# Four stretches between steps of side tasks changed in a two-layer hybrid decoder step

## The chip, the cores and the metric

The kernel runs on one core of a Trainium2 chip. The metric is device time in microseconds (us) of one execution: the median of three runs for the kernel before.

## What is computed

One inference step of a decoder with two layers, for a prompt of 1024 positions and 8 sample rows, here side by side as T = 1032 columns, with D = 1024 channels in fp32. The core of the reference:

```
def layer(x, c, pos, s_ret, conv_buf, w_ada, b_ada, g_mix, w_in, ...):
    mod = jax.nn.silu(c) @ w_ada + b_ada
    sh1, sc1, gt1, sh2, sc2, gt2 = jnp.split(mod, 6, axis=-1)
    h = modulate(rmsnorm(x, g_mix), sh1, sc1)
    p = h @ w_in                       # q, k, v, g: 4 heads x 128;  u, vv: 4 groups x 128
    ...
    o, s_new = retention(q, k, v, s_ret)       # chunks of 128: S = g*S + k^T v, o = att v + q S
    o_ret = silu(g) * groupnorm(o)
    o_gm, v_rows = chunk_gmlp(gelu(u), gelu(vv), w_s, b_s, gmlp_ln_gain)
    x = x + gt1 * (concat([o_ret, o_gm]) @ w_out)
    h2 = modulate(rmsnorm(x, g_ffn), sh2, sc2)
    a, buf_new = causal_dwconv(h2 @ w_up, conv_buf, conv_w, conv_b)
    f = silu(a[..., :D_FF]) * a[..., D_FF:]    # D_FF = 2048
    x = x + gt2 * (f @ w_down)
```

## The kernel before

**Matmuls.** Channels lie on the partitions. Every large product is made of 128x128 weights against three column chunks of 344. For precision each operand is split into a high and a low part (hi, lo), and a product is three matmuls into the same PSUM bank: L262 hi·hi, L263 hi·lo, L264 lo·hi, here called a triple. There are 3840 triples in the program, and places in it are told below as the number of triples ahead of them. A weight piece comes by DMA as `raw` (two pieces ahead), ACT makes `hi` of it (L212) and DVE `lo` (L221). Three functions run the triples: `unit()` for one output tile of an input or up projection (24 triples: 3 chunks by 8), `joint()` for the first two tiles after a norm (48), and `partial()` for the output and down projections, whose inputs are products of earlier units. ACT's and DVE's evacuations of a unit (L291, L292) and the split of weights (`W.ahead()`) are issued from inside these loops.

**Side tasks.** Everything else is done by generators in a queue (`Side`, shown below): the retention heads (v, k, q, o), the gMLP groups, the FFN's convolution and product, the norms, and ada (the modulation's products, L573 for the DMA and L589 for PE). Each `yield x` ends a step and says how many modelled microseconds later the next is due. `tick(us)` moves the modelled clock on and runs at most two steps that are due, in the queue's order; ada has a lower priority than heads, norms a higher one. `unit()` and `partial()` call it every three triples with KB = 1.31, `joint()` after each triple with KB/3. So the program order on every engine is fixed when the kernel is built, by these numbers; each engine then works through its own queue in that order. Slots in SBUF (23, one size) and PSUM banks (8) are taken from rotating pools, in program order too.

**The tasks that the change touches.**
- `norm()` (L441 to 468): a norm's side of a joint. `add_squares()` adds up squares on DVE (L377), `inv_rms()` multiplies them by a matrix of ones (L395), then the inverse root goes over DRAM and comes back as R, by which DVE multiplies (L317, L292). The stretch at L444 stands between L377 and L395, for the norms that have a `wait` (the second and the third chunk of a joint).
- `Head.task_k()` (L715 to 756): k is rotated, transposed on PE and copied to `kt` on ACT (L729); after the stretch at L732 PE multiplies kt by vt (L742). The q and o tasks of the head follow: `qm` (L767), the products L772, L782, then o and the mixing of heads (L814, L817, L830, L849).
- `Ffn.evac_b().rest()` (L931 to 940): the second half of an FFN step. After L932 come the three taps of the convolution (L911, L915), after L934 the product with the first half's SiLU (L935, on DVE; L925 is the SiLU), `ahi` (L937, ACT), and 2.5 later `alo` (L939, DVE). ahi and alo are the inputs of the down projection's `partial()`.

Of the kernel before, what the change touches and what calls it, by code (L numbers as in the profile page):

```python
# [90 lines left out]
def tile_hybrid_decoder_step(  # L91
# [321 lines left out]
    def to_dram(w):  # L413
        rd = dp.tile([4, QW], F32, tag="rd", name=f"rd{count[0]}")
        nc.gpsimd.dma_start(out=rd, in_=w[0:128:32])
        return rd

    def from_dram(o, rd):

        nc.sync.dma_start(out=o, in_=rd.rearrange("j n -> (j n)")[0:o.shape[1]].partition_broadcast(128))  # L420
# [17 lines left out]
    def norm(c, hold, R, A, B, gate=None, dma=True, wait=0):  # L438

        n = CW if c < 2 else CW - NB  # L440
        if wait:  # L441
            yield wait
        rows = add_squares(c, hold, gate)
        yield 5 if wait else 4  # L444
        w = inv_rms(rows)
        yield 4
        if dma:
            rd = to_dram(w)
        if c == 2 or not dma:
            r = spread(w, (3,) if dma else range(4))  # L450
        yield 1
        o = R[:, c * CW:c * CW + n]
        if dma:
            from_dram(o, rd)
        else:
            nc.scalar.activation(out=o, in_=r[:, 0:n], func=ACTF.Copy)
        if c == 2:
            q = small([128, KT, NB], "gs")
            ss = slice(SEQ, T)
            rb = r[:, CW - NB:CW].unsqueeze(1).to_broadcast([128, KT, NB])  # L460
            nc.vector.tensor_tensor(out=q, in0=XS, in1=rb, op=ALU.mult)
            nc.vector.tensor_tensor(out=q, in0=q, in1=A[:, :, 1:9], op=ALU.mult)
            nc.vector.tensor_tensor(out=q, in0=q, in1=B[:, :, 1:9], op=ALU.add)
            nc.scalar.activation(out=Hh[:, :, ss], in_=q, func=ACTF.Copy)
            nc.vector.tensor_tensor(out=Hl[:, :, ss], in0=q, in1=Hhf[:, :, ss], op=ALU.subtract)
# [193 lines left out]
    class Head:  # L659
# [61 lines left out]
        def task_k(self, sw):  # L721
            h = self.h
            yield 3
            self.rope(self.k, sw)
            kt = slot("kt")
            yield 5

            def ev(hf, ps):
                nc.scalar.activation(  # L729
                    out=kt[:, hf * 512:(hf + 1) * 512], in_=ps, func=ACTF.Identity, scale=dec[:, h:h + 1])  # L730
            halves(self.k, ev)
            yield 4  # L732
            vb = self.vb[:, 0:1024]
            vb8 = vb.rearrange("p (b e) -> p b e", b=8)
            nc.gpsimd.tensor_tensor(
                out=vb8, in0=vb8, in1=self.k[:, SEQ:T].unsqueeze(2).to_broadcast([128, 8, 128]), op=ALU.mult)
            self.S = slot("S")
            S = self.S[:, 0:1024].rearrange("p (c e) -> p c e", c=8)
            pss = [sps(), sps()]
            for q in range(8):  # L740
                t = slice(q * 128, (q + 1) * 128)
                nc.tensor.matmul(  # L742
                    pss[q // 4][:, q % 4 * 128:(q % 4 + 1) * 128], kt[:, t], self.vt[:, t], start=True, stop=True)
            for hf, ps in enumerate(pss):
                for q in range(4):
                    c = hf * 4 + q
                    kv = ps[:, q * 128:(q + 1) * 128]
                    if c == 0:
                        nc.vector.tensor_copy(S[:, 0], kv)
                    else:  # L750
                        nc.vector.scalar_tensor_tensor(
                            out=S[:, c], in0=S[:, c - 1], scalar=GAMMA[h] ** 128, in1=kv, op0=ALU.mult, op1=ALU.add)
            yield 3.5
            nc.gpsimd.dma_start(out=rp_o[self.l, h], in_=S[:, 7])
            s0 = self.S0[:, 0:1024]
            nc.vector.scalar_tensor_tensor(out=s0, in0=s0, scalar=GAMMA[h], in1=vb, op0=ALU.mult, op1=ALU.add)
            yield 2
            nc.gpsimd.dma_start(
                out=rs_o[self.l, h], in_=self.S0[:, 0:1024].rearrange("p (b e) -> p b e", b=8))
# [126 lines left out]
    class Ffn:  # L886
# [41 lines left out]
        def evac_b(self, ps, p):  # L928
            ac = self.conv(ps, 16 + p)

            def rest():  # L931
                yield 5  # L932
                c1, c2 = self.c1, (yield from self.taps(ac, 16 + p))
                yield 4  # L934
                nc.vector.tensor_tensor(out=c2[:, 0:T], in0=c2[:, 0:T], in1=c1[:, 0:T], op=ALU.mult)  # L935
                hi, lo = slot("ahi", F32R), slot("alo", F32R)
                nc.scalar.activation(out=hi[:, 0:T], in_=c2[:, 0:T], func=ACTF.Copy)  # L937
                yield 2.5
                nc.vector.tensor_tensor(  # L939
                    out=lo[:, 0:T], in0=c2[:, 0:T], in1=hi.bitcast(F32)[:, 0:T], op=ALU.subtract)  # L940
                self.f[p] = (hi, lo)
            self.tasks[p] = side.add(rest(), after=[self.first])
# [315 lines left out]
```

## Time and profile before

| | us |
|---|---|
| median of 3 runs | 2059.28 (2058.11 to 2060.38) |
| the profiled execution | 2058.09 |
| its span | 2056.4 |
| PE busy | 2021.2 (98%) |
| DVE busy | 1230.2 (60%) |
| ACT busy | 669.4 (33%) |

The program is bound by PE, which works through its matmuls back to back. A part of the profile lists the times in which PE stood idle by the operation that it waited for; a timeline shows the instructions of an engine with their start and length, and in square brackets how long the engine was idle ahead of one and what ended it. Matmul ends are modelled: each is drawn 0.32 long though one starts every 0.16, so distances are best read from start to start.

### The profile page before, as it was taken

To read this page: it belongs to the slowest core of one execution; us is meant where nothing else is said; L and a number is where in the kernel's file an instruction comes from. 1 tells how busy PE (TensorE), PEld (TensorE's weight loads), DVE (VectorE), ACT (ScalarE), POOL (GpSimd) and SP (SyncE) were. 2 spreads that over 40 slices of the span, in tenths; PEclk is the share of its full clock that TensorE was granted. 3 is DMA by queue.
4 is the path that set the end of the run, shared out by engine and by line. 5 is a ranking of instruction groups with operands and counts; after the bars stand their busy time and mean duration, and the time that the engine had idled before them with its cause. 6 is when DMAs were issued, how large, how long until landed. Compare 5 with 4: busy or idle time off the path is not lost.

```text
span 2056.4 us, 32662 instructions
## 1 busy us (share of the span) xinstructions
PE 2021.2 (98%) x13837; PEld 1966.2 (96%) x13837; DVE 1230.2 (60%) x2562; ACT 669.4 (33%) x930; POOL 71.0 (3%) x155
## 2 busy tenths in 40 slices
PE   8999999999999999999999999999999999999997
PEld 5999999999899999999999999999999999999997
DVE  4456635686556456454784674458857655645476
ACT  4422123234412222414343331332442332241432
POOL 0000000000000000000000000000100000000001
PEclk9999999999999999999999999999999999999999
DMA  8444311112544211010122211121121111111002
GB/s 312 170 145 145 113 64 52 55 58 106 183 167 170 83 52 52 32 62 32 56 68 77 74 42 61 54 74 38 46 70 52 42 41 52 52 31 62 31 35 84
DMA packets 51889, 164.32 MB, mean 80 GB/s; under 512 B 6864, under 2 KB 14384, under 8 KB 51744
## 3 DMA queue, kind: packets, MB, share of 16 engines
q1 hardware_dynamic: 47616, 151.22, 21.6%
q0 software_dynamic: 3728, 10.50, 1.4%
q8 instruction: 108, 1.77, 0.3%
q10 hardware_dynamic: 400, 0.53, 0.1%
q14 instruction: 37, 0.30, 0.0%
HBM read 152.88 MB, written 9.61 MB: 79 GB/s over the span
## 4 chain that ended last, share of the span: by engine, by line
PE 88%; DVE 7%; ACT 3%; DMA 1%; issue 1%; SPq 0%; DVEq 0%; ACTq 0%
PE big L262 27%; PE big L263 26%; PE big L264 26%; PE side L589 2%; PE side L629 1%; DVE Hl L435 1%; DVE X L536 1%; DMA ada<-in_w_ada 1%; PE side L742 1%; PE side L772 1%; PE side L793 1%; PE side L872 1%; DVE lo L221 1%; PE side L795 1%; ACT sq L366 1%
## 5 line engine op out<-in xcount | busy, mean ns | idle before, releaser
L262 PE MATMUL big<-Hh,hi 128*128 128x344 f32 (+1 forms) x2688 | 871.2, 324 | 0.0
L263 PE MATMUL big<-Hl,hi 128*128 128x344 f32 (+1 forms) x2688 | 861.5, 321 | 0.2 <-DVE Hl L435 0.2
L264 PE MATMUL big<-Hh,lo 128*128 128x344 f32 (+1 forms) x2688 | 861.4, 320 | 0.0
L262 PEld LDWEIGHTS big<-Hh,hi 128*128 128x128 f32 x2688 | 506.1, 188 | 15.8 <-issue 13.9
L263 PEld LDWEIGHTS big<-Hl,hi 128*128 128x128 f32 x2688 | 506.5, 188 | 0.7 <-DVE Hl L435 0.4
L264 PEld LDWEIGHTS big<-Hh,lo 128*128 128x128 f32 x2688 | 506.7, 189 | 0.0
L221 DVE TENSOR_TENSOR lo<-raw,hi 128x1024 fp32r<-128x1024 f32 x160 | 195.5, 1222 | 293.5 <-ACT hi L212 293.1
L292 DVE TENSOR_TENSOR row<-big,R 128x344 f32<-128x344 f32 x309 | 157.9, 512 | 310.2 <-ACT wb L291 193.6
L335 DVE SCALAR_TENSOR_TENSOR X<-big,mod,X 128x344 f32<-128x344 f32 x384 | 211.0, 571 | 70.8 <-PE big L264 68.6
L263 PE MATMUL big<-alo,hi 128*128 128x344 f32 x768 | 245.2, 319 | 2.3 <-DVE alo L939 2.3
L262 PE MATMUL big<-ahi,hi 128*128 128x344 f32 x768 | 246.6, 321 | 0.0
L264 PE MATMUL big<-ahi,lo 128*128 128x344 f32 x768 | 245.4, 319 | 0.0
L291 ACT ACTIVATE wb<-big 128x1 f32<-128x1 f32 x103 | 17.3, 168 | 567.5 <-PE big L264 567.5
L212 ACT ACTIVATE hi<-raw 128x1024 fp32r<-128x1024 f32 x160 | 165.6, 1046 | 12.4 <-PE side L589 7.2
L911 DVE SCALAR_TENSOR_TENSOR c<-row,pars,c 128x1032 f32<-128x1032 f32 x128 | 164.3, 1286 | 0.3
L262 PEld LDWEIGHTS big<-ahi,hi 128*128 128x128 f32 x768 | 144.3, 188 | 3.3 <-issue 1.6
L263 PEld LDWEIGHTS big<-alo,hi 128*128 128x128 f32 x768 | 144.4, 188 | 2.6 <-DVE alo L939 2.6
L264 PEld LDWEIGHTS big<-ahi,lo 128*128 128x128 f32 x768 | 144.3, 188 | 0.0
L262 PE MATMUL big<-hi,hi 128*128 128x344 f32 x384 | 124.0, 323 | 0.0
L264 PE MATMUL big<-hi,lo 128*128 128x344 f32 x384 | 122.7, 319 | 0.0
L263 PE MATMUL big<-lo,hi 128*128 128x344 f32 x384 | 122.6, 319 | 0.0
L937 ACT ACTIVATE ahi<-c 128x1032 fp32r<-128x1032 f32 x32 | 34.2, 1069 | 221.9 <-DVE c L935 201.5
(178 smaller groups left out, 1748.6 us busy)
## 6 DMA issues: line engine op xcount, KB each, us to landing
ada<-in_w_ada SPq DMA_DIRECT2D x96, 512.0 KB, 5.1
raw<-in_w_up SPq DMA_DIRECT2D x64, 512.0 KB, 3.5
raw<-in_w_in SPq DMA_DIRECT2D x48, 512.0 KB, 3.5
raw<-in_w_down SPq DMA_DIRECT2D x32, 512.0 KB, 3.4
raw<-in_w_out SPq DMA_DIRECT2D x16, 512.0 KB, 3.5
S<-in_s_ret POOLq DMA_DIRECT2D x8, 512.0 KB, 3.8
vb<-vd SPq DMA_DIRECT2D x8, 512.0 KB, 4.7
out_rs<-S POOLq DMA_DIRECT2D x8, 512.0 KB, 3.0
```

Source lines behind the costliest of these rows:

```text
L212: nc.scalar.activation(out=hi[:, 0:1024], in_=self.raw[i][:, 0:1024], func=ACTF.Copy)
L221: nc.vector.tensor_tensor(out=lo[:, 0:1024], in0=self.raw.pop(i)[:, 0:1024], in1=self.split[i][0].bitcast(F32)[:, 0:1024], op=ALU.subtract)
L262: nc.tensor.matmul(out, whi, rhi, start=start, stop=False)
L263: nc.tensor.matmul(out, whi, rlo, start=False, stop=False)
L264: nc.tensor.matmul(out, wlo, rhi, start=False, stop=stop)
L292: nc.vector.tensor_tensor(out=a[:, cols(c)], in0=ps[:, 0:CW], in1=R[:, cols(c)], op=ALU.mult)
L335: nc.vector.scalar_tensor_tensor(out=x, in0=ps[:, 0:CW], scalar=gt[:, m, 0:1], in1=x, op0=ALU.mult, op1=ALU.add)
L366: nc.scalar.activation(out=o, in_=x, func=ACTF.Square)
L435: late.append(lambda x=x, a=a, m=m: nc.vector.scalar_tensor_tensor(out=Hl[:, m, s], in0=x, scalar=a, in1=Hhf[:, m, s], op0=ALU.mult, op1=A ...
L589: nc.tensor.matmul(ps[32 * j:32 * j + 32, 0:256], scond[:, k, :], w[:, j * 256:(j + 1) * 256], start=(k == 0), stop=(k == KT - 1), tile_po ...
L911: nc.vector.scalar_tensor_tensor(out=c[:, off:off + T], in0=a[:, 0:T], scalar=wt, in1=c[:, off:off + T], op0=ALU.mult, op1=ALU.add)
L937: nc.scalar.activation(out=hi[:, 0:T], in_=c2[:, 0:T], func=ACTF.Copy)
```

## The change

Four numbers, each a stretch between two steps of a task:

```diff
@@ norm() @@
         rows = add_squares(c, hold, gate)
-        yield 5 if wait else 4
+        yield 6.5 if wait else 4
         w = inv_rms(rows)
@@ Head.task_k() @@
             halves(self.k, ev)
-            yield 4
+            yield 7.5
             vb = self.vb[:, 0:1024]
@@ Ffn.evac_b().rest() @@
-                yield 5
+                yield 3.5
                 c1, c2 = self.c1, (yield from self.taps(ac, 16 + p))
-                yield 4
+                yield 2.5
                 nc.vector.tensor_tensor(out=c2[:, 0:T], in0=c2[:, 0:T], in1=c1[:, 0:T], op=ALU.mult)
```

No instruction is added or removed; the order in the queues changes. Three places show how.

ACT's queue, head 3 of the first layer. L667 to L669 evacuate q, L729 copies the transposed k to kt in two halves, L212 makes a weight's high part. Before:

```order
L291 ACTIVATE wb_3254<-big_3343 128x1
L667 ACTIVATE row_3288<-row_3288,wb_3254 128x1032
L668 ACTIVATE qs_3370<-row_3288 64x1032
L669 ACTIVATE qs_3370<-row_3288 64x1032
L729 ACTIVATE kt_3307<-side_3374,dec 128x512
L729 ACTIVATE kt_3307<-side_3375,dec 128x512
L212 ACTIVATE hi_3397<-raw_3093 128x1024
```

After:

```order
L291 ACTIVATE wb_3245<-big_3317 128x1
L667 ACTIVATE row_3288<-row_3288,wb_3245 128x1032
L668 ACTIVATE qs_3370<-row_3288 64x1032
L669 ACTIVATE qs_3370<-row_3288 64x1032
L212 ACTIVATE hi_3385<-raw_3068 128x1024
L729 ACTIVATE kt_3327<-side_3398,dec 128x512
L729 ACTIVATE kt_3327<-side_3399,dec 128x512
```

The weight's high part has come ahead of the two copies. On PE, the transposes of k go from triple 528 to 534 and the products L742 that use kt from 540 to 552.

PE's queue in the first layer's joint (triples 768 to 816), around the second of the three L395. Before:

```order
L262 MATMUL big_4792<-Hh,hi_4601 128x346
L263 MATMUL big_4792<-Hl,hi_4601 128x346
L264 MATMUL big_4792<-Hh,lo_4634 128x346
L395 MATMUL side_4815<-sq_4528,ones_m 32x86 x12
L262 MATMUL big_4792<-Hh,hi_4601 128x346
L263 MATMUL big_4792<-Hl,hi_4601 128x346
```

After:

```order
L264 MATMUL big_4792<-Hh,lo_4634 128x346
L262 MATMUL big_4820<-Hh,hi_4530 128x344
L263 MATMUL big_4820<-Hl,hi_4530 128x344
L264 MATMUL big_4820<-Hh,lo_4599 128x344
L262 MATMUL big_4820<-Hh,hi_4530 128x344
L263 MATMUL big_4820<-Hl,hi_4530 128x344
L264 MATMUL big_4820<-Hh,lo_4599 128x344
L395 MATMUL side_4827<-sq_4528,ones_m 32x86 x12
L262 MATMUL big_4820<-Hh,hi_4530 128x344
```

The product has gone from ahead of the chunk's last triple to behind the next chunk's second, from triple 783 to 786; the third goes from 793 to 796.

DVE's queue in the second layer's FFN, ahead of the partial product after the third step. L221 makes a weight's low part, L292 evacuates a chunk, L911 and L915 are taps, L935 the product, L939 alo. Before:

```order
L221 TENSOR_TENSOR lo_14752<-raw_14536,hi_14732 128x1024
L292 TENSOR_TENSOR row_14758<-big_14722,R_13793 128x344
L911 SCALAR_TENSOR_TENSOR c_14716<-row_14654,pars,c_14716 128x1032
L935 TENSOR_TENSOR c_14614<-c_14614,c_14516 128x1032
L911 SCALAR_TENSOR_TENSOR c_14716<-row_14654,pars,c_14716 128x1032
L292 TENSOR_TENSOR row_14758<-big_14760,R_13793 128x344
L221 TENSOR_TENSOR lo_14808<-raw_14635,hi_14754 128x1024
L939 TENSOR_TENSOR alo_14785<-c_14614,ahi_14784 128x1032
```

After:

```order
L292 TENSOR_TENSOR row_14658<-big_14689,R_13793 128x344
L935 TENSOR_TENSOR c_14615<-c_14615,c_14516 128x1032
L221 TENSOR_TENSOR lo_14756<-raw_14536,hi_14733 128x1024
L292 TENSOR_TENSOR row_14762<-big_14723,R_13793 128x344
L939 TENSOR_TENSOR alo_14739<-c_14615,ahi_14738 128x1032
L911 SCALAR_TENSOR_TENSOR c_14717<-row_14658,pars,c_14717 128x1032 x2
L292 TENSOR_TENSOR row_14762<-big_14764,R_13793 128x344
L221 TENSOR_TENSOR lo_14809<-raw_14635,hi_14758 128x1024
```

The product L935 has come ahead of an L221 and an L292 that stood in front of it, and alo (L939) ahead of the two taps and the second L221.

Besides, the q and o tasks of a head come 6 triples later (head 3: 12; head 1 of the second layer: 9), and the ada tasks in the first layer's mixing 9 to 21 triples sooner, in its FFN 6 to 9.

## Rows read from the trace of the kernel before

**Rows 1.** The page, busy time and granted clock in 40 slices:
```profile
PE 2021.2 (98%) x13837; PEld 1966.2 (96%) x13837; DVE 1230.2 (60%) x2562; ACT 669.4 (33%) x930; POOL 71.0 (3%) x155
...
PEclk9999999999999999999999999999999999999999
```
**Rows 2.** PE's waits: who waited for what; us in total, times, longest:
```profile
PE side L589 <- DMA ada<-in_w_ada: 9.5, 3, 7.8
PE side L742 <- ACT kt L729: 4.6, 2, 2.3
PE side L408 <- DVE rw L360: 3.9, 1, 3.9
PE side L395 <- DVE sq L377: 3.2, 3, 1.1
PE big L263 <- DVE alo L939: 2.3, 1, 2.3
PE side L998 <- DVE wm L993: 1.5, 1, 1.5
PE side L782 <- DVE qm L767: 1.0, 1, 1.0
```
**Rows 3.** Timeline of PE, head 3: start, us, instruction [idle before <- releaser]:
```profile
355.74 0.32 PE L264 MATMUL big<-Hh,lo 128*128 128x344 f32 x1
358.39 2.05 PE L742 MATMUL side<-vt,kt 128*128 128x128 f32 x16 [2.34 <-ACT kt L729]
```
**Rows 4.** Timeline of PE, ada products in the first layer's mixing:
```profile
160.33 0.32 PE L264 MATMUL big<-Hh,lo 128*128 128x344 f32 x1
160.57 0.64 PE L589 MATMUL side<-ada,scond 128*32 128x256 f32 x8
```
**Rows 5.** Timeline of ACT, the same stretch as rows 3:
```profile
354.31 1.16 ACT L667 ACTIVATE row<-row,wb 128x1032 f32<-128x1032 f32 x1 [2.09 <-DVE row L292]
...
357.65 1.26 ACT L729 ACTIVATE kt<-side,dec 128x512 f32<-128x512 f32 x2
358.81 1.06 ACT L212 ACTIVATE hi<-raw 128x1024 fp32r<-128x1024 f32 x1
```
**Rows 6.** Timeline of PE, first layer's joint:
```profile
488.99 0.32 PE L264 MATMUL big<-Hh,lo 128*128 128x346 f32 x1
490.30 0.65 PE L395 MATMUL side<-sq,ones_m 128*32 128x86 f32 x24 [0.99 <-DVE sq L377]
```
**Rows 7.** Timeline of PE, second layer's FFN:
```profile
1557.58 0.31 PE L262 MATMUL big<-ahi,hi 128*128 128x344 f32 x1
1560.18 0.42 PE L263 MATMUL big<-alo,hi 128*128 128x344 f32 x1 [2.29 <-DVE alo L939]
```
**Rows 8.** Timeline of DVE, the same stretch:
```profile
1557.77 1.21 DVE L221 TENSOR_TENSOR lo<-raw,hi 128x1024 fp32r<-128x1024 f32 x1
1558.90 1.22 DVE L939 TENSOR_TENSOR alo<-c,ahi 128x1032 fp32r<-128x1032 f32 x1
```
**Rows 9.** Timeline of DVE, head 0 of the first layer:
```profile
125.03 0.52 DVE L292 TENSOR_TENSOR row<-big,R 128x344 f32<-128x344 f32 x1 [2.25 <-PE side L772]
125.46 0.17 DVE L767 COPY qm<-row 128x8 f32<-128x8 f32 x1
```
**Rows 10.** Ada's DMA (L573), 100 to 320 us: who waited, us and times; landing:
```profile
  PE side L589: 1.7, 2
...
DMA to landing us min/median/max: 3.4/4.5/7.6
```
**Rows 11.** Timeline of PE, second layer's mixing:
```profile
1216.45 0.27 PE L849 MATMUL side<-ident,row 128*128 128x128 f32 x1
```
**Rows 12.** Timeline of ACT, the same stretch:
```profile
1214.77 1.16 ACT L830 ACTIVATE row<-row,wb 128x1032 f32<-128x1032 f32 x1 [0.80 <-DVE row L292]
```
**Rows 13.** Timeline of DVE, second layer's FFN, first steps:
```profile
1541.48 1.22 DVE L221 TENSOR_TENSOR lo<-raw,hi 128x1024 fp32r<-128x1024 f32 x1 [4.24 <-ACT hi L212]
```
**Rows 14.** Timeline of ACT, the same steps:
```profile
1526.31 1.28 ACT L925 ACT_TABLE_LOAD   x1
...
1539.45 1.05 ACT L925 ACTIVATE c<-c 128x1032 f32<-128x1032 f32 x1
...
1545.90 0.17 ACT L291 ACTIVATE wb<-big 128x1 f32<-128x1 f32 x1 [0.52 <-PE big L264]
```

## The prediction

> **What bounds the kernel now.** I read the page's first two parts first. The matmul engine PE is busy 98% of the span at full granted clock in all 40 slices, VectorE (DVE) 60%, ScalarE (ACT) 33% [rows 1]. So only two things can shorten this kernel: fewer matmuls, or fewer moments in which PE stands still. The change leaves every instruction in place and alters only when some of them are queued, so the whole question is which of PE's waits it removes and which it makes. The second view is therefore PE's own list of waits [rows 2]. It sums to some 26 us. Of these, 3.9 us (L408) at the end, 1.5 us (L998) and most of the 9.5 us on ada (7.8 in one wait) lie at the head and tail of the program, where no edited task runs. I looked only at the rest, and then asked for the stretch around each one, on PE and on the engine it waited for.
>
> One correction to the view. PE starts a big matmul every 0.16 us, but the profile draws each as 0.32 long, so the wait it prints is measured from an end that overlaps the next step. From 355.74 to 358.39 are 2.65 us; less the 0.24 that the step from a big matmul to a side product takes (160.33 to 160.57 [rows 4]) that is 2.41, where the view says 2.34 [rows 3]. From 1557.58 to 1560.18 less a step of 0.16 is 2.44, where it says 2.29 [rows 7]. So I add about 0.1 to each wait. A triple (the three matmuls L262 to L264) is 3 x 0.158 = 0.47 us, and a tick of a unit (three triples) 1.42 us of PE's time. The side tasks count in ticks of 1.31, so a stretch of 4 is 4 ticks (12 triples), 7.5 is 6 ticks (18), 3.5 is 3, 2.5 is 2; in a joint, with a tick per triple, 5 is 12 triples and 6.5 is 15.
>
> **Part 1: products of k and v later (L732, 4 to 7.5).** The products L742 of head 3, once per layer, wait for the transposed k that ACT copies out of PSUM (kt, L729): 4.6 us in two waits [rows 2]. ACT shows why: the copy stands in its queue behind the evacuation of q (L667, L668, L669), so it starts at 357.65 and the first of its two halves comes out at about 358.3 [rows 5]. The edit sets the products 6 triples further behind the transposes, and in the new order the transposes stand 6 triples later as well. So L742 is due 12 triples, 5.7 us, later: about 355.98 + 5.7 = 361.7. In the new order the split of a weight (L212) also stands ahead of the copy: 357.65 + 1.06 for L212 + 1.26 for both copies = 360.0 [rows 5]. Slack 1.7 us; both waits go: **-4.6 - 0.2 = -4.8 us**. The six other heads do not wait now, and get more room. What follows in a head (its q and o tasks) slides 6 to 12 triples, and with it the turn of the ada tasks, which have a lower priority and move 9 to 21 triples ahead in the first layer.
>
> **Part 2: sums of squares in the joint later (L444, 5 to 6.5).** In three of the joints the product that adds the squares up (L395) waits for the DVE sum (L377), 3.2 us in three waits, the longest 1.1 [rows 2, 6]. It is moved 3 triples, 1.42 us, later. With 0.1 added the longest wait is 1.2, so a margin of 0.2 us is left there and 0.35 at the joint shown (due 488.99 + 0.24 + 1.42 = 490.65, ready 490.30 [rows 6]). **-3.2 - 0.3 = -3.5 us**, on thin margins. What comes behind it (the inverse root, and R's way over DRAM) is set back by 1.42 less what L395 waited, 0.2 to 0.4 us per joint. The last of these products now stands 20 triples, 9.5 us, ahead of the joint's end, and R is first used by DVE behind that, so I cost it at nothing; with that cover gone it would be 0.2 to 0.4 three times, up to 1 us.
>
> **Part 3: the FFN's second half sooner (L932 5 to 3.5, L934 4 to 2.5).** Only one of the 32 steps waits: the partial product at 1557.58 needs alo, and its DVE operation L939 stands behind a weight's lower half (L221, 1557.77 to 1558.98) and ends at 1560.12: 2.3 us [rows 2, 7, 8]. With the edit the product (L935) is queued 9 triples sooner and alo 12, ahead of the L221 that is now in front of it. 12 triples are 5.7 us, so it would end at 1554.4 if DVE were free; an L221 of 1.21 may run in front of it, so 1555.6 at the latest, where 1557.7 is needed. **-2.3 - 0.15 = -2.45 us.** The other 31 steps do not wait and gain nothing.
>
> **Part 4: what else slides.** At 125 us the product with the sample rows' queries (L782) waits 1.0 us for qm (L767), a small copy behind an L292 on DVE [rows 2, 9]. Its task comes 6 triples later (2.8 us), and in the new order the three k rope products of head 1 come ahead of it on DVE. At 1.22 us each (an operation of the same shape, L939 [rows 8]) they take 3.7 us. I put their start some 2 us before L767's old place at 125.5, so that L767 comes at about 127.5; L782 was due at about 125.0 and is due 2.8 later, plus a group of ada products now ahead of it (0.6 [rows 4]): 128.4. This is the least certain of the terms. Gone: -1.1. Two ada products (L589) wait for their weights' DMA in the first layer's mixing, 1.7 us together; the longest landing there took 7.6 us, the median 4.5 [rows 10]. They are issued 9 to 21 triples sooner, at places where slots are free: -1.8.
>
> Sum of parts: 4.8 + 3.5 + 2.45 + 1.1 + 1.8 = 13.65 us.
>
> **What is given back.** The trace of before does not show the new neighbours, so I bound this from both sides. Below: nothing, since the same matmuls run and each moved one finds its input. Above: there are five places where the order puts a side product within 0.5 us of its input by my reckoning. Two are ada products in the first layer, now 9 triples behind the previous group; three are the transposes of mix (L849) behind an evacuation (L830). The nearest row for these is L849 at 1216.45, where L830 ended at 1215.93, 0.5 us of slack [rows 11, 12]; at the new places it has 0 to 0.3. If every one waited as long as the waits of this size do now (1.0 [rows 2]), it would be 5 us. I take 0.5, since the nearest row shows slack and no wait. Net 13.15, and 2058.1 - 13.15 = 2044.9 for the profiled run. That run is 1.2 below the median of the three (2059.28), so the median becomes **2046.1 us**.
>
> [...] At the first steps of each FFN the product L935 is now queued ahead of the next L221 and L292, and it waits for SiLU (L925), which ended at 1540.50 [rows 14], while DVE had been idle since 1537.24. L221 waited for the split (L212) until 1541.48 in any case and ended at 1542.70 [rows 13]; behind L935 (1.2) it would end at 1542.9, 0.2 later. The unit before ended near 1545.9, where its last column is copied (L291 [rows 14]), so the weight is needed from about 1545.7: a cover of 3.0 us. A blocked head of DVE's queue costs nothing here as long as it is shorter than that. [...]
>
> **Rivals.** (1) Only the three waits that the edited lines name go, and the ada and qm waits stay or reappear elsewhere: 4.8 + 3.5 + 2.45 = 10.75 saved, 2048.5. For it: those two depend on DVE's and DMA's timing in a stretch I could only reconstruct. Against: in the order both producers move away from their consumers. (2) All the thin places wait, 5 us back: 2059.3 - 13.65 + 5 = 2050.6. For it: slack of 0 to 0.3 us. Against: five at once. (3) The waits move along with the products (the copy of kt again behind other ACT work, the sums again late since DVE is busier there), and nothing is gained: 2058 to 2060. Against: the order shows what stands ahead of each. (4) Slower: L935 blocks DVE for longer than the 3.0 us of cover in every FFN step, and the next weight's lower half is late. If ACT ran a table load (1.28 [rows 14]) and the splits of two weights (1.06 each [rows 5]) ahead of SiLU, L221 would be 3.4 + 0.2 = 3.6 us later and each of the 32 steps would start 0.6 late: +19.2, with part 3's gain gone 2059.3 - 11.2 + 19.2 = 2067.3. It decides from 3.0 us on. Against it: the one row shows 0.2 of the 3.0 used.
>
> **How the numbers follow.** Forecast 0.62 (2046.1), rival 1 0.17, rival 2 0.12, rival 3 0.05, rival 4 0.04. A measurement of this kernel tells about 0.2%, 4.1 us, from no change: faster is below 2055.2. Forecast and rivals 1 and 2 all lie there, 0.91; 0.02 of it I give to mixtures that end nearer. So faster 0.89, same 0.07, slower 0.04. The range goes from 2044.0 (no give-back, and a little off the two small neighbours of the head) to 2052.0 (rival 2 with rival 1's smallest loss): it leaves out rivals 3 and 4 and a tail of rival 2, under 0.2.
>
> **What would show it.** In the list of PE's waits after the change L742 behind kt, big L263 behind alo, L395 behind L377 and L782 behind qm should be gone, and ada's row should fall to 7.8 in one wait. Part 1 is wrong if kt L729 still stands in the list, part 2 if L395 does with 0.1 to 0.3 each, part 3 if DVE waits on SiLU and a big L264 behind lo L221 appears. A row of L849 behind L830, or of L589 behind ada between 100 and 150 us or later than 200 us, is the give-back. The prediction falls if PE's waits shrink as said and the time does not.

## The result and the profile after

| | before | after |
|---|---|---|
| median, us | 2059.28 (2058.11 to 2060.38) | 2044.55 (2044.12 to 2045.82) |
| the profiled execution | 2058.09 | 2044.70 |
| its span | 2056.4 | 2043.0 |
| PE's waits, sum of the list | 26.2 | 14.6 |

The ratio is 0.9929, with a 95% interval of 0.9917 to 0.9941. Later comparisons, with more runs of the kernel before, put its median at 2057.6 to 2058.5; in the last of them the changed kernel had 2044.71 beside 2057.64, a ratio of 0.9938 (0.9925 to 0.9952). So the gain is 13 to 15 us, and 13.4 between the two profiled executions.

The page of the changed kernel, busy time (to be read against rows 1):

```profile
PE 2019.8 (99%) x13837; PEld 1966.9 (96%) x13837; DVE 1232.0 (60%) x2562; ACT 668.2 (33%) x930; POOL 71.0 (3%) x155
```

The instruction counts are the same, and so is the work of every engine within 2 us. What changed is PE's list of waits; here it is whole (answers to rows 2: us in total, times, longest):

```profile
PE side L589 <- DMA ada<-in_w_ada: 8.9, 2, 8.5
PE side L408 <- DVE rw L360: 4.0, 1, 4.0
PE side L998 <- DVE wm L993: 1.5, 1, 1.5
PE big L263 <- DVE Hl L435: 0.2, 1, 0.2
```

L742, L395, the big L263 behind alo, and L782 are gone, and ada has two waits where it had three. What is left lies in the first 30 us and behind 2000 us, apart from one wait of 0.5. The stretch between, 30 to 2000 us, in one line of each kernel (columns: length, busy time of PE, weight loads, DVE, ACT and POOL with instructions, granted clock, DMA share, GB/s). Before:

```profile
30.00:2000.00 1970.00, 1957.12 (x13355) 1913.26 (x13355) 1182.41 (x2455) 643.66 (x893) 57.02 (x132) 1.00 0.22 76
```

After:

```profile
30.00:2000.00 1970.00, 1969.53 (x13440) 1927.11 (x13439) 1193.58 (x2476) 645.29 (x895) 57.02 (x132) 1.00 0.23 76
```

Before, PE stood idle for 12.9 us of it (1970.00 less 1957.12); after, for 0.5. It now gets through 85 more matmuls in the same 1970 us. So PE's list leaves half a microsecond in this stretch for a further shift of side tasks to win.

The places themselves, on PE, answer rows 3, 6, 7 and the wait for qm. None has a bracket any more:

```profile
358.62 1.95 PE L742 MATMUL side<-vt,kt 128*128 128x128 f32 x16
...
485.02 0.65 PE L395 MATMUL side<-sq,ones_m 128*32 128x86 f32 x24
...
1546.14 0.32 PE L263 MATMUL big<-alo,hi 128*128 128x344 f32 x1
...
129.27 0.67 PE L782 MATMUL side<-S,qm 128*32 128x128 f32 x16
```

Their producers, first ACT, then DVE:

```profile
350.46 1.16 ACT L667 ACTIVATE row<-row,wb 128x1032 f32<-128x1032 f32 x1 [1.67 <-DVE row L292]
...
353.81 1.06 ACT L212 ACTIVATE hi<-raw 128x1024 fp32r<-128x1024 f32 x1
354.78 1.25 ACT L729 ACTIVATE kt<-side,dec 128x512 f32<-128x512 f32 x2
```

```profile
483.83 1.65 DVE L377 TENSOR_TENSOR sq<-sq,sq 128x688 f32<-128x688 f32 x2
...
1542.08 1.23 DVE L939 TENSOR_TENSOR alo<-c,ahi 128x1032 fp32r<-128x1032 f32 x1
```

kt is complete at 356.03 and used at 358.62: 2.6 us to spare. alo ends at 1543.31 and is used at 1546.14: 2.8 to spare. L377's second half ends at 485.48, L395's first use is of an earlier part; the dependency of the first product was met 0.33 us ahead of 485.02, where 0.35 was foreseen.

### The profile page after: what moved, and what is told of

The parts are those of the page before. It is cut to its first block, busy times and chain, and to the rows that moved or that the text cites. A ratio compares the mean times of both kernels' runs of the same rounds, so it can differ in the third digit from the quotient of the medians.

```text
span 2043.0 us, 32668 instructions
## 1 busy us (share of the span) xinstructions
PE 2019.8 (99%) x13837; PEld 1966.9 (96%) x13837; DVE 1232.0 (60%) x2562; ACT 668.2 (33%) x930; POOL 71.0 (3%) x155
## 4 chain that ended last, share of the span: by engine, by line
PE 98%; DMA 1%; issue 0%; SPq 0%; POOL 0%; DVE 0%; POOLq 0%; ACT 0%
PE big L262 30%; PE big L263 30%; PE big L264 30%; PE side L589 2%; PE side L629 1%; DMA ada<-in_w_ada 1%; PE side L872 1%; PE side L742 1%; PE side L793 1%; PE side L772 1%; PE side L795 1%; PE side L395 0%; PE side L998 0%; PE side L408 0%; PE side L782 0%
## 5 line engine op out<-in xcount | busy, mean ns | idle before, releaser
L263 PE MATMUL big<-Hl,hi 128*128 128x344 f32 (+1 forms) x2688 | 861.7, 321 | 0.2 <-DVE Hl L435 0.2
L264 PE MATMUL big<-Hh,lo 128*128 128x344 f32 (+1 forms) x2688 | 861.5, 321 | 0.0
L263 PEld LDWEIGHTS big<-Hl,hi 128*128 128x128 f32 x2688 | 506.4, 188 | 0.7 <-DVE Hl L435 0.4
L264 PEld LDWEIGHTS big<-Hh,lo 128*128 128x128 f32 x2688 | 506.6, 188 | 0.0
L292 DVE TENSOR_TENSOR row<-big,R 128x344 f32<-128x344 f32 x309 | 158.0, 513 | 342.3 <-ACT wb L291 210.0
L221 DVE TENSOR_TENSOR lo<-raw,hi 128x1024 fp32r<-128x1024 f32 x160 | 195.7, 1223 | 242.6 <-ACT hi L212 242.6
L264 PE MATMUL big<-ahi,lo 128*128 128x344 f32 x768 | 245.5, 320 | 0.0
L263 PE MATMUL big<-alo,hi 128*128 128x344 f32 x768 | 245.3, 319 | 0.0
L212 ACT ACTIVATE hi<-raw 128x1024 fp32r<-128x1024 f32 x160 | 166.3, 1046 | 2.1 <-DMA raw<-in_w_in 1.4
L911 DVE SCALAR_TENSOR_TENSOR c<-row,pars,c 128x1032 f32<-128x1032 f32 x128 | 164.7, 1290 | 2.2 <-issue 0.6
L263 PEld LDWEIGHTS big<-alo,hi 128*128 128x128 f32 x768 | 144.3, 188 | 0.0
L264 PEld LDWEIGHTS big<-ahi,lo 128*128 128x128 f32 x768 | 144.2, 188 | 0.0
L264 PE MATMUL big<-hi,lo 128*128 128x344 f32 x384 | 122.7, 320 | 0.0
L263 PE MATMUL big<-lo,hi 128*128 128x344 f32 x384 | 122.7, 319 | 0.0
L901 ACT ACTIVATE row<-row,wb 128x1032 f32<-128x1032 f32 x64 | 74.2, 1159 | 40.4 <-DVE row L292 38.8
```

Source lines behind the costliest of these rows:

```text
L212: nc.scalar.activation(out=hi[:, 0:1024], in_=self.raw[i][:, 0:1024], func=ACTF.Copy)
L221: nc.vector.tensor_tensor(out=lo[:, 0:1024], in0=self.raw.pop(i)[:, 0:1024], in1=self.split[i][0].bitcast(F32)[:, 0:1024], op=ALU.subtract)
L263: nc.tensor.matmul(out, whi, rlo, start=False, stop=False)
L264: nc.tensor.matmul(out, wlo, rhi, start=False, stop=stop)
L292: nc.vector.tensor_tensor(out=a[:, cols(c)], in0=ps[:, 0:CW], in1=R[:, cols(c)], op=ALU.mult)
L901: nc.scalar.activation(out=a[:, 0:T], in_=a[:, 0:T], func=ACTF.Identity, bias=b)
```

## The experiments

The theory: PE is never the engine that is late; each edit removes the wait that it aims at, us for us, and nothing else stands behind those waits. One edit, that of the k and v products, carries two more waits with it, since the heads' later tasks and ada's turn hang on it. The rivals are in each expectation. In the tables of waits the columns are those of rows 2.

### Each edit alone

**Only L732.**

```diff
             halves(self.k, ev)
-            yield 4
+            yield 7.5
```

> Only the stretch between the transposes of k and the products of k and v is changed (L732, 4 to 7.5). Theory (the saving is the sum of the waits of PE that each edit removes, and this edit alone also removes the waits for qm and for ada in the first layer, because it slides the heads' later tasks): L742's 4.6 us, L782's 1.0 and ada's 1.7 are gone from PE's list, 0.5 for ada comes back as in the changed kernel; L395's 3.2 and alo's 2.3 stay. About 7.3 us faster than before: 2052.0. Rival (qm and ada have nothing to do with this edit): only L742's waits go, 4.8 us, 2054.5, with L782 and 1.7 of ada still in the list. Second rival (a removed wait only lets PE run into the next late producer): a new wait behind L742's old place, and less than 4 us gained.

Measured: 2050.86 us beside 2058.47 of the kernel before, ratio 0.9963 (0.9950 to 0.9976): 7.6 us less. PE's waits, the rows that matter:

```profile
PE side L589 <- DMA ada<-in_w_ada: 8.3, 2, 7.9
...
PE side L395 <- DVE sq L377: 3.2, 3, 1.1
PE big L263 <- DVE alo L939: 2.4, 1, 2.4
```

L742 and L782 are not in the list and ada is down to the wait at the head and 0.4. The other two edits' waits stand untouched. So this one number gives over half of the gain, about 5 of it where it aims and 2 to 3 by what slides behind it. The profiled execution (2051.80) is the slowest of its five, and has a stretch of lower clock in it, told in the last section.

**Only L444.**

```diff
-        yield 5 if wait else 4
+        yield 6.5 if wait else 4
```

> Only the stretch ahead of the sums of squares in the joint is changed (L444, 5 to 6.5). Theory: L395 behind L377 (3.2 us, three waits) is gone, every other row of PE's list stays; 3.5 us faster, 2055.8. Rival (R comes later by as much, and DVE's multiplication by R passes it on): 1 us less, 2056.8, with a new wait on DVE's row or on R.

Measured: 2056.44, ratio 0.9991 (0.9982 to 1.0000): 2.0 us less. L395 has left the list and no row for R, DVE or a DMA has taken its place, so the mechanism is as expected; the time fell by less than the 3.4 us that went, and the interval (0 to 3.7 us) holds either. In the profiled execution, read from start to start against that of before, the three waits gave 3.5 us, as foreseen, and 1.6 were lost at another place: at 357 to 363 us the granted clock was 0.72 (last section). That the other executions lost by the same is not shown.

**Only L932 and L934.**

```diff
-                yield 5
+                yield 3.5
                 c1, c2 = self.c1, (yield from self.taps(ac, 16 + p))
-                yield 4
+                yield 2.5
```

> Only the FFN's second half is sooner (L932 5 to 3.5, L934 4 to 2.5). Theory: the one wait of a big L263 for alo (2.3 us) is gone and nothing else changes; 2.45 us faster, 2056.8. Rival (DVE's queue is held up by the product that waits for SiLU, and the lower halves of the weights are late): no gain or a loss, with a big L264 behind lo L221 in PE's list.

Measured: 2055.91, ratio 0.9985 (0.9975 to 0.9994): 2.6 us less. The wait for alo is gone, the rest of the list is that of before, and no L264 waits for a lower half. Together the three alone give 7.6 + 2.0 + 2.6 = 12.2 us; all at once gave 13 to 15. They add up, within what these medians can tell: no edit needs another, and none takes from another.

### What of L732 acts where

**7.5 for head 3 alone, then for heads 0 to 2 alone.**

```diff
-            yield 4
+            yield 7.5 if h == 3 else 4
```

> The stretch of L732 is 7.5 for head 3 alone, 4 for the others; the other three numbers as before. Here L742 of head 3 goes from triple 540 to 546, and the transposes (528) and all of heads 0 and 1 stay in place. Theory: L742's waits go (due 2.84 us later, where 2.4 was missing), 4.6 to 4.8 us, and L782's 1.0 and ada's 1.7 stay in the list: 2054.5. Rival (the 6 triples that the transposes slid are needed too): 0.5 us or more of each wait stays.

Measured: 2054.96, ratio 0.9984 (0.9974 to 0.9993): 3.5 us less, not 4.8. The list shows what the forecast missed:

```profile
PE side L589 <- DMA ada<-in_w_ada: 9.0, 3, 7.9
...
PE side L849 <- ACT row L830: 1.5, 2, 0.8
...
PE side L782 <- DVE qm L767: 0.9, 1, 0.9
```

L742's 4.6 us are gone and ada and qm stay, as the theory has it. But a wait of L849 for L830 has come, once per layer, at triple 630: of the kind that the prediction calls thin, though not one of the three places that it counted. Its chain on DVE, ACT and PE:

```profile
406.57 1.23 DVE L189 TENSOR_TENSOR lo<-mix,hi 128x1032 fp32r<-128x1032 f32 x1 [1.13 <-ACT hi L188]
407.72 1.40 DVE L876 SCALAR_TENSOR_TENSOR mix<-side,pars,bsb 128x512 f32<-128x512 f32 x2
409.04 0.51 DVE L292 TENSOR_TENSOR row<-big,R 128x344 f32<-128x344 f32 x1
```

```profile
409.58 1.16 ACT L830 ACTIVATE row<-row,wb 128x1032 f32<-128x1032 f32 x1 [2.20 <-DVE row L292]
```

```profile
410.79 0.33 PE L849 MATMUL side<-ident,row 128*128 128x128 f32 x1 [0.77 <-ACT row L830]
```

With head 3's tasks 6 triples later, its mixing (L811, L817, L189) stands on DVE at triple 621, in the same tick as L876, and the evacuation L292 queues behind them. In the changed kernel the shift is 12, the mixing stands at 627, behind that evacuation, and L849 does not wait.

The counterpart:

```diff
-            yield 4
+            yield 4 if h == 3 else 7.5
```

> The counterpart of the kernel that changed head 3 alone: L732 is 7.5 for heads 0 to 2 and 4 for head 3; the other three numbers as before. Theory (qm and ada hang on the heads 0 and 1, kt on the order around head 3): L782's wait is gone and ada's falls by 1.2 or more; L742 of head 3, at triple 546 with the transposes slid to 534 and L212 ahead of the copy, is due at 358.8 where kt's first half comes at 359.35, so 0.5 us stays in each layer; and the two waits of L849 behind L830 (1.5 us) that showed with head 3 alone come here too, since DVE's order around triple 621 is the same. PE's list 26.2 - 1.0 - 1.2 - 3.6 + 1.5 = 21.9, and the time 4.5 us below before. Rival (L849's waits belong to something else in that kernel): no L849 in the list, 6 us below.

Measured: 2053.96, ratio 0.9979 (0.9969 to 0.9988): 3.9 us less, where 4.5 was expected. qm is gone, ada is down to 8.7 in two waits, and L849 waits 1.6 us in two, so that wait does come from head 3's place and not from something else in that kernel. The 0.5 us that was to stay with L742 did not: its copy of kt, behind L212, was in time.

**One tick less, and one more.**

```diff
-            yield 7.5
+            yield 5.5
```

> The changed kernel with 5.5 in place of 7.5 at L732, one tick less: transposes at 531, L742 of head 3 at 546, qm at 159. Theory: L742 is due at 358.8, kt's first half behind L212 comes at 359.35: 0.5 us in each layer; L849 behind L830 1.5 us as in the two kernels in which head 3's products stand at 546; qm's wait is gone (3 triples are 1.42 us where 1.06 was missing) or left with 0.4 if the rope products of the next head come ahead of it. 2.5 to 3.5 us slower than the changed kernel: 2047 to 2048. Rival (any stretch over 5 does, the exact value is of no account): the changed kernel's time within 0.5 us.

Measured: 2052.93 beside 2057.90; 8.4 us slower than the changed kernel, and both the theory's 3 and the rival's 0 are wrong. The list:

```profile
PE side L589 <- DMA ada<-in_w_ada: 12.8, 4, 8.0
PE side L408 <- DVE rw L360: 4.0, 1, 4.0
PE side L849 <- ACT row L830: 2.4, 3, 0.8
```

L849 is as foreseen, L742 and qm are gone, but three ada waits of 4.7 us in all have come. The order shows what may be behind it: the first issue for a group of ada weights is at triple 201, as in the kernel before, and the mixing of head 0, which stood at 198, is now at 201 in the same tick and ahead of it, so that the slots which it frees come later still. In the changed kernel that issue stands at 189, ahead of the mixing (204).

```diff
-            yield 7.5
+            yield 9.0
```

> The changed kernel with 9 in place of 7.5 at L732 (7 ticks, not 6). Theory (an ada product waits where the DMA of its weights is issued behind the mixing of a head, whose last DVE operation, L189, frees the slots): around triple 195 the issue stands ahead of head 0's mixing (207) and nothing waits; head 1's mixing and L189 now stand at 270, the same place as an ada issue that is used at 279. The mixing's DVE work takes about 3.5 us from there and a landing 3.4 us or more, where 9 triples give 4.3: one wait of 2 to 3 us near triple 279, and no L849 in the list, since L830 (264) is 9 triples ahead of L849 (273). 2 to 3 us slower than the changed kernel, 2046.5 to 2047.5. Rival (later is better throughout, or the ada waits are mere scatter of the DMA): the changed kernel's time within 0.7 us and no ada wait over 0.5 apart from the one at the head.

Measured: 2056.18 beside 2057.95, ratio 0.9988 (0.9978 to 0.9998): nearly the whole gain is lost again, 11.5 us where 2 to 3 were expected. Ada's row reads 13.6 us in five waits. The wait that was expected, at triple 279, did not come; two of 1.5 and 0.6 us came near 229 us, at triple 297, and the largest was another. (A wait of 1.0 us of L782 is in the list too, for no producer that the profile names.)

```profile
130.32 0.64 PE L589 MATMUL side<-ada,scond 128*32 128x256 f32 x8 [3.31 <-DMA ada<-in_w_ada]
```

Its weights were issued by SP from 122.89 us on; in the changed kernel SP began the same four at 119.40. The piece that the product waited for was issued at 126.87 and landed 3.4 us later, as short as any landing of rows 10, so the issue was late and not the transfer. What SP's queue waited for (us, times, longest; 122 to 128 us) and DVE's row:

```profile
SPq L573 <- DVE lo L221: 5.3, 1, 5.3
SPq L573 <- DVE row L676: 3.6, 1, 3.6
```

```profile
121.63 1.23 DVE L221 TENSOR_TENSOR lo<-raw,hi 128x1024 fp32r<-128x1024 f32 x1 [4.48 <-ACT hi L212]
```

With 7.5 the three rope products (L674 to L676) stand at triple 150, ahead of this L221, and run from 116.62 to 120.25 while DVE would be idle. With 9 they stand at triple 153, behind it: DVE idles for 4.48 us, the rope products run from 123.20 to 126.84, and the issues that wait for DVE's work come that much later. So "later is better" is wrong by this run, and so was my account of which issue would be late.

**One slot fewer.**

```diff
-NSLOT = 23
+NSLOT = 22
```

> The changed kernel with 22 slots in the pool of SBUF tiles in place of 23; nothing else is changed. Theory (the ada weights wait for a free slot, not for bandwidth): every issue of ada and raw comes later by about the time to the next release, ada waits of 1 us and more come back in the first layer's mixing, and other rows of PE's list stay as they are: 2 to 6 us slower than the changed kernel. Rival (their DMA is slow by itself): no difference over 0.7 us.

Measured: 2052.21, 7.7 us slower than the changed kernel. Besides 1.5 us of ada waits the list has a new row:

```profile
PE side L782 <- POOL vb L735: 3.0, 1, 3.0
```

The list names POOL, which turns v to vb (L735), and vb's own DMA was not what it waited for: issued at 119.79 (in the changed kernel at 116.27), it took 4.7 us to land, where it took 5.0 there, and was in place 9.6 us ahead of L782. L735 waited for a rope product on DVE, and DVE had stood still before it. Here are POOL and then DVE:

```profile
132.13 1.89 POOL L735 TENSOR_TENSOR vb<-vb,row 128x1024 f32<-128x1024 f32 x1 [18.29 <-DVE row L676]
```

```profile
126.58 1.23 DVE L221 TENSOR_TENSOR lo<-raw,hi 128x1024 fp32r<-128x1024 f32 x1 [5.92 <-PE side L589]
```

In the changed kernel the same L221 begins at 121.19, after 0.93 us of idle in which it waits for hi. With 22 slots it is released by an ada product on PE, which fits a slot that this product sets free; the trace does not name the slot. So one slot fewer reaches PE here by way of DVE's queue: what stands behind a blocked L221 comes late, and L782 with it. As for the ada waits, the piece awaited was issued 1.1 us later than in the changed kernel and took 5.3 us to land where it took 4.6 there, so late issue and slow transfer both have a part. That the number of slots sets these waits is shown, by 7.7 us; that the transfers' own length has no part in them is not. A kernel with 24 slots was not run.

### How far the other two numbers reach

**The sums 1 triple later, not 3.**

```diff
-        yield 6.5 if wait else 4
+        yield 5.6 if wait else 4
```

> The changed kernel with 5.6 in place of 6.5 at L444: the sums of squares' product is 1 triple later than in the kernel before, not 3. Theory (the wait is the missing distance, us for us): each of the three waits of L395 shrinks by 0.47 and comes to 0.5 to 0.7, 1.6 us in PE's list; 2.0 us slower than the changed kernel, 2046.6. Rival (the wait is set by something that moves along, such as DVE's queue behind later work): the waits are 3.2 as before, or gone altogether.

Measured: 2046.79, 2.1 to 2.2 us slower than the changed kernel, as expected to 0.2.

```profile
PE side L395 <- DVE sq L377: 1.8, 3, 0.6
```

3.2 us at no triple, 1.8 at one, nothing at three: each triple takes 0.47 off each wait. The wait is a missing distance and nothing else.

**The FFN's second half as early as it goes.**

```diff
-                yield 3.5
+                yield 1
                 c1, c2 = self.c1, (yield from self.taps(ac, 16 + p))
-                yield 2.5
+                yield 1
```

> The changed kernel with 1 and 1 in place of 3.5 and 2.5 at L932 and L934: the FFN's second half another 6 to 9 triples sooner. Theory (the second half waits for nothing late, and the cover of the weights' lower halves is 3 us): the first tap (L911) now stands ahead of an L221 and an L292 and waits for ACT's L902 by up to 3 us, PE's list does not change, the time is that of the changed kernel within 0.5 us. Rival (strict order of DVE's queue: an operation queued too soon holds up the lower halves behind it): a big L264 behind lo L221 in PE's list, and 0.5 us or more lost in many of the 32 steps, 10 us or more.

Measured: 2044.84, the changed kernel's time to 0.3. PE's list is the same row by row. On DVE the operations queued too soon do wait now (us, times, longest), rows which the changed kernel does not have:

```profile
DVE c L911 <- ACT acol L904: 52.8, 23, 2.6
...
DVE c L911 <- ACT c L902: 8.7, 4, 2.6
```

61 us of a blocked queue in 27 waits, none over 2.6 us, and PE feels nothing of it. Over the FFN's weights of that execution the lower halves are ready 2.99 us before their first use at the tightest place (1532.14 to 1535.12), and 6.2 us at the median, so no wait was as long as the cover. DVE does stand still at an operation queued too soon, and the price here is zero up to this length, 2.6 us; this run does not show at which length it would begin, but with 22 slots a block of 5.9 us, at another place, cost PE 3.0.

### One wait put back

**The changed kernel with the FFN's stretches of before, and the changed kernel beside it.**

```diff
-                yield 3.5
+                yield 5
                 c1, c2 = self.c1, (yield from self.taps(ac, 16 + p))
-                yield 2.5
+                yield 4
```

> The changed kernel with the FFN's stretches put back to 5 and 4, so that one wait of 2.3 us (a big L263 for alo, at about 1550) is all that it has more. Theory (a wait of 2 us and more costs its length, and in some executions 1.4 to 1.7 us besides, because the granted clock falls behind it): the times lie 2.5 us above the changed kernel's, some of them 3.9 to 4.1 above, so that they spread by 1.5 us and more; in the profiled execution either every stretch behind 1552 is at clock 1.00, or one of 4 to 6 us behind the wait is at 0.55 to 0.75. Rival (the wait costs its length and the scatter is the ada DMA's): 2.5 us above, and no more spread than the changed kernel has.

> The changed kernel itself beside the one with the FFN's stretches put back, on the same chip, for the spread of its times. It has no wait over 0.6 us between 30 and 2000 us. Theory: its times lie within 1.5 us of each other apart from single strays, and the clock is 1.00 in every stretch between 30 and 2000 us. Rival (the clock falls without a wait as well): a spread of 3 us and more, as the kernel before has.

Measured: with the wait put back 2046.12, 2046.76, 2046.87, 2047.51 and 2049.22, median 2046.87; the changed kernel 2044.52, 2044.64, 2044.71, 2045.72 and 2045.93, median 2044.71. The wait of 2.4 us costs 2.2, so undoing this edit gives back what doing it alone gained. One run of five lies 4.5 above, which is what the theory of the clock wants, but one run is no proof, in the profiled execution the clock did not fall, and on record the mean granted clock is 0.994 in that run as in the fastest of the five. No wait but the one at the head and 0.5 us of ada is in the changed kernel's second profile either.

## Why the prediction was right, point by point

The forecast was 2046.1 and the measured median 2044.55.

- **Part 1, kt: right.** Both waits went. From the step ahead of L742, start to start, 6.23 us over its 8 places became 1.11 over 7: 5.0 where 4.8 was foreseen. The slack was 2.6 and not 1.7: ACT's chain ran about a microsecond sooner against PE than I had it, since L667 waits for an L292 on DVE (the bracket in its row above), and that comes out sooner in the new order.
- **Part 2, the sums: right.** 6.68 us ahead of the 13 products became 3.24: 3.4, foreseen 3.5. The margin at the joint shown was 0.33 us, foreseen 0.35. R's delay cost nothing.
- **Part 3, alo: right.** 2.4 us, foreseen 2.45; L939 ends at 1543.31, 2.8 us early.
- **Part 4, qm and ada: right in what moves, and about right in size.** qm went (1.06 us), with L767 at 127.07 and L782 at 129.27, where I had 127.5 and 128.4. Ada's row did not fall to 7.8 in one wait, as the sign said, but to 8.9 in two: the wait at the head grew to 8.5, which costs nothing (the first big matmul starts 0.3 us sooner), the two in the mixing at 162 and 216, 1.7 us together, went, and one of 0.5 came:

```profile
125.28 0.64 PE L589 MATMUL side<-ada,scond 128*32 128x256 f32 x8 [0.47 <-DMA ada<-in_w_ada]
```

  That is the 0.5 which I gave back, and between 100 and 150 us, where the signs had it; but this group of ada is not one of those that moved. It stands at triple 159 in both kernels. Before, L772 and L782 stood ahead of it; now they stand behind, so it is due at 124.17, while its second piece, issued at 119.84, lands at 125.24. The experiment with L732 alone shows that both hang on that edit, as the working had it.
- **The thin places: right by luck of the value.** In the changed kernel the list names none of them. Three of the L849 (374.72, 1176.50 and 1374.39) do start only 0.05 us after their L830 ends, and the step ahead of them is 0.21 to 0.22 where it is 0.16 to 0.17 elsewhere, so there the cover was just gone, at 0.05 each. And the experiments show that they are real: L849 waits 0.8 us per layer as soon as head 3 slides by 6 triples and not 12. Rival 2 was the right worry, at a place which I had not counted. And the price of an ada wait was far too low in the expectations of 5.5 and 9: 4.7 us and 5.6 us of them came, where I had none and 2 to 3.
- **Rival 4: its premise was wrong.** I let the product L935 of a step wait for the SiLU that ends at 1540.50 before [rows 14]. That is the SiLU of the next step. The product's own is the one before it, and a step's second half is queued only behind its first (`after=[self.first]`), so L935 cannot stand ahead of its SiLU. In the changed kernel (the rows on ACT, then on DVE) the product shown follows its SiLU by 8.5 us and waits for nothing, and over all 32 steps the distance is never under 7.2:

```profile
1516.62 1.07 ACT L925 ACTIVATE c<-c 128x1032 f32<-128x1032 f32 x1
```

```profile
1526.18 1.22 DVE L935 TENSOR_TENSOR c<-c,c 128x1032 f32<-128x1032 f32 x1
```

  The block of DVE that the rival needs can only come from the taps (L911), and those it took stretches of 1 to bring about, with waits of 2.6 us at the longest. The 4.24 us of idle ahead of L221 [rows 13] were the split's, as the row says, and held up nothing: the L292 behind it had its input only from about 1541.9.
- **The sum and the step to the median.** The list fell by 11.6 us, the spans by 13.4; the forecast for the profiled execution was 13.15. The list holds the wait at the head, which grew by 0.7 and costs nothing. Between 30 and 2000 us PE's idle time fell by 12.4 (12.9 to 0.5); with 0.1 for each of the eight waits by which the list is shorter there, and the 0.3 by which the first big matmul starts sooner, that is 13.5, and the sum closes. The 1.5 us by which the median came out lower than forecast is the step from profile to median: I carried over that the profiled execution of before lay 1.2 below its median, and that of the changed kernel lies at it (2044.70 and 2044.55). A term that the sum did not have at all is what a wait can cost behind its end; it is told in the last section. There too the first reading of the prediction is set right, that the clock was full in all 40 slices and only two things could shorten this kernel: a 9 in the page stands for 90% and more of a slice of 51 us, and a stretch of a few us at a lower clock does not show in it: the first slice prints a 9 too, with 0.53 at 9 to 20 us.

## What to carry to other kernels

Where one engine is busy 98% and its waits are few, take the list of its waits, go to each, and ask how many of its own steps it would have to come later, or its producer sooner; here a wait then went us for us (each of L395's three by 0.47 a triple), and edits at different places added up (12.2 us one by one, 13 to 15 together). A delay shifts everything that hangs on the task, so count the neighbours too: here the same edit at 5 ticks, 6 and 7 gave 2052.9, 2044.6 and 2056.2 us, and only the order of the queues told why, as far as it is told, never the size of the number. Look for the place where two moved tasks fall into one tick, and for DMA issues behind the work that frees their buffers (with 9 at L732 one such wait was 3.31 us).

## What was not expected: the clock behind a wait

Six of the experiments have stretches of a few us between 30 and 2000 us in which the granted clock is under 1.00, each directly behind a wait. The windows behind the waits, for L732 alone (the wait for alo, ending at 1552.51), for L444 alone (the wait for kt), for 5.5 at L732 (ada waits of 1.8 and 2.5 us), for 9 at L732 (3.31 us, ending at 130.32, and 1.47 and 0.64, ending at 230.05), and for 22 slots (3.03 us, ending at 134.15); the columns are those of the windows above. L732 alone:

```profile
1552.00:1556.00 4.00, 3.49 (x13) 3.50 (x14) 2.17 (x5) 2.70 (x4) 0.00 (x0) 0.57 0.47 131
```

L444 alone:

```profile
357.00:363.00 6.00, 5.45 (x29) 5.45 (x30) 3.63 (x10) 2.02 (x3) 0.00 (x0) 0.72 0.25 83
```

5.5 at L732:

```profile
162.00:166.00 4.00, 4.00 (x21) 3.19 (x18) 1.89 (x3) 0.00 (x0) 0.00 (x0) 0.59 0.95 364
219.00:224.00 5.00, 4.88 (x25) 4.47 (x26) 0.67 (x1) 1.06 (x1) 0.00 (x0) 0.66 0.62 229
```

9 at L732:

```profile
130.00:137.00 7.00, 6.68 (x52) 5.95 (x53) 3.96 (x5) 0.28 (x1) 1.89 (x1) 0.76 0.33 128
137.00:144.00 7.00, 7.00 (x60) 6.22 (x59) 1.04 (x2) 5.07 (x7) 0.00 (x0) 1.00 0.21 77
230.00:236.00 6.00, 5.95 (x32) 5.54 (x33) 1.15 (x2) 0.38 (x1) 0.00 (x0) 0.72 0.00 0
```

22 slots, the windows and three matmuls of the slow stretch:

```profile
134.00:141.00 7.00, 6.85 (x39) 6.47 (x40) 1.48 (x4) 0.45 (x2) 0.02 (x1) 0.54 0.01 2
141.00:148.00 7.00, 7.00 (x65) 6.25 (x64) 1.04 (x2) 6.46 (x8) 0.00 (x0) 1.00 0.27 77
```

```profile
135.64 0.49 PE L263 MATMUL big<-Hl,hi 128*128 128x346 f32 x1
135.93 0.49 PE L264 MATMUL big<-Hh,lo 128*128 128x346 f32 x1
136.22 0.49 PE L262 MATMUL big<-Hh,hi 128*128 128x346 f32 x1
```

There a big matmul starts every 0.29 us where it is 0.16 elsewhere, and the granted clock is 0.54 over the 7 us from 134 to 141, where it is 1.00 over the 7 behind them.

What such a stretch costs is read best from the same work with such a stretch and without. From the awaited L263 to triple 3000, L732 alone and 7.5 for heads 0 to 2 alone, with a slow stretch (the latter 0.83 over 1550 to 1560), took 80.5 and 80.6 us; four kernels without one took 78.9 to 79.1. From L742 to triple 760, L444 alone took 121.4, and the kernel before and the FFN's edit alone 119.8. So a stretch costs 1.5 to 1.6 us; its length times what is missing of the clock (4 x 0.43, 6 x 0.28) says 1.7, a little too much. With 22 slots it is about twice as much, 7 x 0.46 = 3.2 by that reckoning. With 1.6 a stretch the accounts against the changed kernel nearly close. For 5.5 at L732 the list of waits is 20.9 against 14.6, 6.3 more; two stretches are 3.2; and 0.1 for each of 5 more waits makes 10.0, where the spans differ by 10.6. For 9 at L732: 5.7 + 3.2 + 0.4 = 9.3, of 10.2. For 22 slots: 4.7 + 3.2 + 0.2 = 8.1, of 8.7. Without the clock, 3 to 4 us of each would have no cause.

It does not follow every wait. Of the twelve waits of 2.3 to 2.4 us in the profiled executions of before, of the single edits, of the two head variants and of the one put back, three were followed by a slow stretch and nine were not, those of the kernel before among the nine. Of the ada waits (1.8 and 2.5, 3.3, 1.5 with 0.6 right behind) and the 3.0 for vb, all five were. Whether a wait of 2.3 us brings one seems to be chance, and that would account for the spread of the kernel before (2056.1 to 2061.9 in over 60 runs, beside 2044.1 to 2045.9 in nine runs of the changed kernel) and for the 2049.22 of the kernel with one wait put back; no run here ties a single slow time to a stretch, so this part stays a supposition. The mean granted clock on record speaks for it only in part: of 69 runs of the kernel before the seven slowest, 2060.5 to 2061.9, are the seven at 0.993, but those at 0.996 and 0.997 are slower than those at 0.995.

The kernel before has such stretches at both ends as well, 0.53 at 9 to 20 us and 0.50 behind 2047, where the prediction read a full clock; the changed kernel still has both, 0.59 at 9 to 20 us and 0.50 behind 2036. Whether a higher clock there would shorten the kernel, as a third way, no run here shows.
